# A recorded instruction list with its own list scheduler in place of the framework's, in a fused attention, pooling and memory step

## The chip, the cores and the metric

The kernel is written in Bass/Tile and runs on one core of one Trainium2 chip. Its five instruction streams are PE (TensorE: matmuls and transposes; the profile shows its weight loads apart, as PEld), DVE (VectorE), ACT (ScalarE), POOL (GpSimd) and SP (SyncE, which here only issues DMAs). Each stream is executed in order; between streams an instruction waits on semaphores. What counts is the device time of one execution in microseconds (us).

## The reference, cut to what matters

One layer of a streaming encoder, for a prompt of 1024 frames and a running stream of 64 frames, model width 1024:

```python
h = rmsnorm(x, g_norm) @ w_in                  # q k v gf zf u gp qm gm
F = cumsum(log_sigmoid(zf + b_f))              # forget values, one per head and row
s = q @ k.T * SCALE + F[q] - F[k]; s[k > q] = NEG
fox_o  = softmax(s) @ v                        # 8 heads of 64
pool_o = (window_mean(u, (2, 4, 8, 16)) - u) @ w_pool * pool_scale
mk, mv = split(rmsnorm(mem, g_mem) @ w_mem_kv) # 256 memory tokens
mem_o  = softmax(qm @ mk.T * SCALE) @ mv       # 4 heads of 64
cat = [silu(gf) * fox_o, silu(gp) * pool_o, silu(gm) * mem_o]
y = rmsnorm(x + cat @ w_out, g_final)
```

The 64 frames of the stream (the "sample") attend to 512 cached keys and to themselves. Besides `y`, the keys, values, forget values, memory keys and values and the last rows of `u` are outputs. All is float32.

## The kernel before, in words

**Numbers.** Every large product is made with three matmuls: an operand is split into a high part, rounded to the format fp32r, and the rest (`hi`, `lo`), and hi·hi + hi·lo + lo·hi are added in PSUM (`mm`, L78; `mm3`). ACT makes the high part, DVE or POOL the rest.

**Stages.** (1) Inside `with st`, activations `xT` are loaded and split into `xh`/`xl` in three column chunks, `CH` (256, 512 and 320 columns: prompt and sample together), values are projected with the weights `wv` and stored to the output `v_o`, the forget values are summed (`f_chain1` to `f_chain3`, which leave them in the DRAM tiles `gpd` and `gsd`), and the memory keys and values are made. (2) Twenty projections, each of 128 output rows: four for `q`, four for `k`, four gates `gf`, two `u`, two gates `gp`, two `qm` and two gates `gm` (as a pair, `gmx0`). `load_w` fetches 512 KB of weights into `wr` (two buffers in pool `wp`) and `split_w` makes `whi` and `wlo`; `proj_chunk` adds 24 matmuls into one bank `pp` for each chunk, and an evacuation writes the result to DRAM: `q` to `qd`, `k` to the output `kT_o`, gates to `gated`. `u` stays on the chip. (3) Attention, head by head. `fox_load(h)` reads the head's keys back from `kT_o` and the cache into `kl` and splits them into `ks` (ACT L518, POOL L519), and reads the values into `vraw` and splits them into `vs`. Then one `fox_sample` and four `fox_unit`s of 256 rows: load the bias `nb` from `gpd` (the sample's from `gsd`), add the mask to its last 256 columns (`bm`, POOL), load `qraw` from `qd` and split it into `qh`/`ql`, score matmuls into a bank `s`, add the bias and take the running minimum on DVE (L637), exponential on ACT (L552), divide on DVE (L558), transpose on PE into a bank `pt` (L654), split into `phi` (ACT L563) and `plo` (DVE L564), multiply with `vs` into a bank `o`, and store to the DRAM tile `catd`. Memory heads (`mem_*`) are the same without bias and with 256 keys. (4) `pool_mix(0)` and `(1)`: window sums of `u` on POOL and DVE, five chunks each, and three short matmuls per chunk. (5) `load_wout` loads the output weights in eight pieces and splits them into `wh`/`wl` in the space of `xh`/`xl` (L938); `out_prep` reads `catd` and `gated`, multiplies them and splits the product into `chi`/`clo`; `out_tile` does the output projection, the residual and the last norm of one tile of 128 rows, in the order 8 (the sample), 0, 1, ..., 7.

**Banks and buffers.** PSUM pools `pp` (projections and output), `ps` (scores), `pt` (transposes) and `po` (products) have two banks each. A tile that is asked for takes the oldest buffer of its name, and waits until that one's users are done.

**What sets the order.** The program is written as generators that are stepped against each other. Attention goes through the list `ATT` and after each piece steps a list of fill work, until its cost has caught up with a due value:

```python
FILL = "q0 k0 q1 k1 u0 qm0 q2 k2 q3 k3 qm1 u1 gf0 gf1 gf2 gf3 gp0 gp1 gmx0"
ATT = "f0 f1 f2 f3 m0 m1 m2 m3 f4 f5 f6+f7"
R1, R2, LEAD0, SIDE = 1.25, 2.4, 7.0, 6
```

`R1` and `R2` (for the last group, heads 6 and 7 together) are fill per attention cost; every `SIDE` pieces one chunk of `pool_mix` is stepped. Behind `FILL` stand `load_wout` and the output tiles. That program order is then rescheduled by the framework, `tile.TileContext(nc, schedule_with_timeline_sim=True)`, which chooses from a simulated timeline the order in which each engine gets its instructions.

Of the kernel before, what the change touches and what calls it, by code (L numbers as in the profile page):

```python
# [14 lines left out]
P = 128  # L15
# [10 lines left out]
BIG = 3.0e38  # L26
WARM = 10
CH = [(0, 256), (256, 512), (768, 320)]
LAST = (2, 1, 0)
TQ, TK, TGF, TU, TGP, TQM, TGM = 0, 4, 8, 12, 14, 16, 18  # L30


@with_exitstack
def tile_hymba_step(
# [6 lines left out]
    nc = tc.nc  # L41
    PSUM = bass.MemoryType.PSUM

    cp = ctx.enter_context(tc.tile_pool(name="cp", bufs=1))
    dram = ctx.enter_context(tc.tile_pool(name="dram", bufs=1, space=bass.MemoryType.DRAM))
    pp = ctx.enter_context(tc.tile_pool(name="pp", bufs=2, space=PSUM))
    ps = ctx.enter_context(tc.tile_pool(name="ps", bufs=2, space=PSUM))
    pt = ctx.enter_context(tc.tile_pool(name="pt", bufs=2, space=PSUM))
    po = ctx.enter_context(tc.tile_pool(name="po", bufs=2, space=PSUM))
    big = ctx.enter_context(tc.tile_pool(name="big", bufs=1))  # L50
    wp = ctx.enter_context(tc.tile_pool(name="wp", bufs=2))
    rp = ctx.enter_context(tc.tile_pool(name="rp", bufs=4))
# [3 lines left out]
    fstate = [0, 0.0]  # L56
# [35 lines left out]
    sp = st.enter_context(tc.tile_pool(name="sp", bufs=1))  # L92
# [244 lines left out]

    with st:
        xp = st.enter_context(tc.tile_pool(name="xp", bufs=2))
# [62 lines left out]
        Ts = f_chain1(st.enter_context(tc.tile_pool(name="fp", bufs=1)))  # L402
# [27 lines left out]
        for t in range(2):  # L430
# [12 lines left out]
            nc.sync.dma_start(mv_o[c, :], vr[:, :256])  # L443

    ap_ = ctx.enter_context(tc.tile_pool(name="ap", bufs=2))

    def proj_chunk(w, evac, ci):
        wh, wl = w
        t0, n = CH[ci]
        acc = ppt()  # L450
        trip = []
        for k in range(KT):
            xh, xl = xhi[ci][:, k, :], xlo[ci][:, k, :]
            trip += [(wh[:, k, :], xh), (wh[:, k, :], xl), (wl[:, k, :], xh)]
        mm3(acc[:, :n], trip, 24)
        evac(acc, ci, t0, n)
        return 24 * n / 2400.0

    wq = {}
    tseq = []  # L460

    def get_w(tidx):
        if tidx not in wq:
            wq[tidx] = load_w(wt[tidx], KT, P)
        return wq[tidx]

    def proj(tidx, evac):
        w = get_w(tidx)
        i = tseq.index(tidx)
        for ci in range(3):  # L470
            if ci == 1:
                get_w(tseq[i + 1])
            yield proj_chunk(w, evac, ci)

    def proj2(t1, e1, t2, e2):
        we = [(get_w(t), e) for t, e in ((t1, e1), (t2, e2))]
        for ci in LAST:
            for w, e in we:
                yield proj_chunk(w, e, ci)

    def q_tile(r0):
        def f(acc, ci, t0, n):
            t = row("qr")
            nc.vector.scalar_tensor_tensor(
                t[:, :n], acc[:, :n], SCALE, rb[:, t0 : t0 + n], op0=ALU.mult, op1=ALU.mult
            )
            nc.sync.dma_start(qd[r0 // P][:, t0 : t0 + n], t[:, :n])

        return f

    def k_tile(j):
        def f(acc, ci, t0, n):
            t = row("kr")
            nc.vector.tensor_tensor(t[:, :n], acc[:, :n], rb[:, t0 : t0 + n], op=ALU.mult)
            nc.sync.dma_start(kT_o[j * P : j * P + P, t0 : t0 + n], t[:, :n])

        return f

    def gate_tile(r0):
        def f(acc, ci, t0, n):  # L500
            t = row("gr")
            nc.vector.tensor_tensor(t[:, :n], acc[:, :n], rb[:, t0 : t0 + n], op=ALU.mult)
            th = row("gt")
            nc.scalar.activation(th[:, :n], t[:, :n], AF.Tanh, scale=0.5)
            nc.vector.scalar_tensor_tensor(
                t[:, :n], th[:, :n], 1.0, t[:, :n], op0=ALU.add, op1=ALU.mult
            )
            g, r = divmod(r0, 768)
            nc.sync.dma_start(gated[g][ci][r : r + P, :n], t[:, :n])

        return f
# [91 lines left out]
    def fox_unit(h, c, ks, vs):  # L603
# [16 lines left out]
        for i in (0, 1):  # L620
# [24 lines left out]
            yield 2 * n / 2400.0  # L645
        acc = otile()
        for kp in reversed(range(c + 1)):
# [20 lines left out]
            yield 8 * 0.109  # L668
        finish(acc, par, j * P, 256 * c, 256)

    def fox_sample(h, ks, raw):
# [23 lines left out]
        yield 0.5  # L695
# [11 lines left out]
        yield 1.0  # L707
# [17 lines left out]
    def mem_unit(h, c, km, vm):  # L725
# [12 lines left out]
        yield 0.5  # L738
# [16 lines left out]
        yield 0.9  # L755

    def mem_sample(h, km, raw):
# [22 lines left out]
        yield 0.7  # L780
# [25 lines left out]
    def pool_mix(t):  # L806
        u = UT[t]
        wr = ap_.tile([P, 256], F32, tag="qraw", name=nm("wpr"))
        wh = ap_.tile([P, P], F32R, tag="wph", name=nm("wph"), bufs=1)
        wl = ap_.tile([P, P], F32R, tag="wpl", name=nm("wpl"), bufs=1)  # L810
        nc.sync.dma_start(wr[:, :P], wpool[t])
        nc.scalar.copy(wh, wr[:, :P])
        nc.vector.tensor_tensor(wl, wr[:, :P], wh, op=ALU.subtract)
        al, up = slice(0, P), slice(64, P)
        for a, n, c0 in PM:
# [32 lines left out]
            yield  # L848
            acc = ptt()
# [7 lines left out]
            while b < c0 + n:  # L857
# [4 lines left out]
                b = e  # L862
        done.add(f"w{t}")

    def tl(tidx, mk, *a):
        yield from proj(tidx, mk(*a))

    FILL = "q0 k0 q1 k1 u0 qm0 q2 k2 q3 k3 qm1 u1 gf0 gf1 gf2 gf3 gp0 gp1 gmx0"
    ATT = "f0 f1 f2 f3 m0 m1 m2 m3 f4 f5 f6+f7"
    R1, R2, LEAD0, SIDE = 1.25, 2.4, 7.0, 6  # L870
    SLACK = 12

    cst = [-1]

# [42 lines left out]
    def out_ready(t):  # L917
        return cst[0] >= (0 if t == 8 else t // 2 + 1)
# [26 lines left out]
    def out_tile(t):  # L945
# [8 lines left out]
        if i < 9 and out_ready(order[i]):  # L954
            prep[order[i]] = out_prep(order[i])
# [245 lines left out]
```

## Time and profile before

| quantity | value |
|---|---|
| time, three runs | 671.74, 672.5, 672.58 us; median 672.5 |
| profiled execution | 668.75 us |
| its span, first to last instruction | 667.0 us |
| mean granted TensorE clock | 0.953 of full speed |
| data moved | 93.30 MB, mean 140 GB/s; 110194 packets on the queue that carries nearly all of it |
| loads of `qraw` from `qd` | 48 of 128 KB (q of 128 x 256), and smaller ones for the samples |
| attention units that load `qraw` | 8 heads x 5 and 4 memory heads x 5 |

The profile gives, for one execution, the busy time of each engine, the chain of work that ended last (followed back from the last instruction through what released each step), and the costliest groups of instructions by line. A row of a single instruction reads: start in us, duration in us, engine, line, operation, output<-inputs, sizes, a count where like rows are joined, and in brackets the idle time of the engine ahead of it and what ended that. A row of a stretch reads: start and end, its length, the busy time of each engine with its count of instructions, the mean granted clock, the share of the DMA engines' time, and GB/s. Weight loads (PEld) run beside matmuls of the same engine.

### The profile page before, as it was taken

The page shows a single profiled execution, that of the slowest core. Times are in us where ns is not written, and L with a number is a line of the kernel's source. Part 1 is how long each engine was busy: PE and PEld are TensorE (multiplying, and loading weights), DVE is VectorE, ACT ScalarE, POOL GpSimd, SP SyncE. Part 2 cuts the span into 40 slices and gives each one's busy share as a digit, 9 for nine tenths or more (in the row PEclk, how much of TensorE's full clock was granted, in tenths as well). Part 3 has the DMA queues.
Part 4 walks back from the last instruction along what each step waited for, and adds up shares of the span by engine and source line. Part 5 has one row for each costly group of instructions (what it writes and reads, how often), then busy time and mean ns, then how long its engine had stood idle before and what let it go on. Part 6 is the DMA issues. An engine that isn't in the chain of part 4 may idle for free.

```text
span 667.0 us, 11515 instructions
## 1 busy us (share of the span) xinstructions
PE 589.2 (88%) x3810; PEld 532.8 (80%) x3810; DVE 424.5 (64%) x1124; ACT 307.6 (46%) x713; POOL 214.3 (32%) x285
## 2 busy tenths in 40 slices
PE   8999996959889869998889868889999759999996
PEld 6999895859788769888678757879888648899895
DVE  6957020637778576687688746977877658743434
ACT  5657111525355345355565644745654436522212
POOL 3104513425234242230432413743442244322200
PEclk9999998879899969999899899989999988999999
DMA  8996423554455534623223365356445745665521
GB/s 301 302 316 206 137 88 123 104 136 103 116 111 147 97 110 124 133 78 105 76 56 108 95 128 144 94 131 167 124 122 137 176 134 170 185 195 185 175 95 63
DMA packets 110542, 93.30 MB, mean 140 GB/s; under 512 B 31498, under 2 KB 94930, under 8 KB 110482
## 3 DMA queue, kind: packets, MB, share of 16 engines
q1 hardware_dynamic: 110194, 92.30, 50.4%
q8 instruction: 30, 0.49, 0.3%
q10 hardware_dynamic: 288, 0.27, 0.1%
q14 instruction: 30, 0.25, 0.1%
HBM read 70.68 MB, written 21.86 MB: 139 GB/s over the span
## 4 chain that ended last, share of the span: by engine, by line
DMA 36%; PE 31%; DVE 12%; issue 7%; ACT 6%; POOL 5%; SPq 3%; DVEq 0%; ACTq 0%; POOLq 0%
PE pp L78 23%; DMA nb<-gpd 9%; DMA qraw<-qd 8%; DMA vraw<-out_dram 3%; PE s L78 3%; DMA nat<-in_xn_dram 3%; PE o L78 3%; PE pt L654 2%; DVE P L558 2%; DMA catd<-og 2%; DMA nb<-gsd 2%; DMA wr<-in_wout_dram 2%; ACT P L552 2%; DVE P L637 2%; DVE plo L564 2%
## 5 line engine op out<-in xcount | busy, mean ns | idle before, releaser
L78 PE MATMUL pp<-xh,wlo 128*128 128x256 f32 (+2 forms) x480 | 163.0, 340 | 1.9 <-POOL wlo L158 1.9
L78 PE MATMUL pp<-xh,whi 128*128 128x256 f32 (+2 forms) x480 | 162.8, 339 | 0.1
L78 PE MATMUL pp<-xl,whi 128*128 128x256 f32 (+2 forms) x480 | 162.6, 339 | 0.0
L78 PEld LDWEIGHTS pp<-xh,wlo 128*128 128x128 f32 x480 | 94.7, 197 | 8.8 <-POOL wlo L158 2.4
L78 PEld LDWEIGHTS pp<-xh,whi 128*128 128x128 f32 x480 | 94.7, 197 | 6.8 <-issue 0.3
L78 PEld LDWEIGHTS pp<-xl,whi 128*128 128x128 f32 x480 | 94.6, 197 | 6.1
L552 ACT ACTIVATE P<-P,m 128x128 f32<-128x128 f32 (+8 forms) x72 | 55.9, 776 | 67.3 <-DVE m L637 65.4
L558 DVE TENSOR_SCALAR P<-P,rinv 128x256 f32<-128x256 f32 (+9 forms) x108 | 75.0, 703 | 2.2
L78 PE MATMUL pp<-wh,chi 128*128 128x256 f32 (+1 forms) x208 | 68.4, 331 | 6.6 <-ACT wh L938 5.4
L614 POOL TENSOR_TENSOR bm<-nb,mask 128x256 f32<-128x256 f32 x32 | 25.2, 786 | 151.9 <-DMA nb<-gpd 118.8
L78 PE MATMUL pp<-wl,chi 128*128 128x256 f32 (+1 forms) x208 | 67.7, 328 | 0.5 <-POOL wl L940 0.5
L564 DVE TENSOR_TENSOR plo<-pt,phi 128x512 fp32r<-128x512 f32 (+1 forms) x96 | 60.7, 638 | 11.3 <-ACT phi L563 10.7
L78 PE MATMUL o<-phi,vs 128*128 128x256 f32 x160 | 46.5, 298 | 19.9 <-ACT phi L563 10.3
L78 PE MATMUL pp<-wh,clo 128*128 128x256 f32 (+1 forms) x184 | 59.3, 322 | 0.0
L158 POOL TENSOR_TENSOR wlo<-wr,whi 128x1024 fp32r<-128x1024 f32 x20 | 48.4, 2419 | 31.4 <-ACT whi L157 29.9
L78 PE MATMUL s<-ks,qh 128*128 128x512 f32 (+4 forms) x112 | 42.9, 385 | 15.8 <-DVE m L637 7.9
L563 ACT CAST phi<-pt 128x512 fp32r<-128x512 f32 (+1 forms) x96 | 51.1, 546 | 7.9 <-PE pt L654 6.8
L78 PEld LDWEIGHTS o<-phi,vs 128*128 128x128 f32 x160 | 31.6, 197 | 23.6 <-ACT phi L563 9.2
L78 PEld LDWEIGHTS pp<-wh,chi 128*128 128x128 f32 x208 | 40.7, 196 | 10.6 <-ACT wh L938 5.8
L78 PE MATMUL o<-plo,vs 128*128 128x256 f32 x160 | 43.8, 297 | 3.9 <-DVE plo L564 3.9
L654 PE MATMUL pt<-ident,P 128*128 128x128 f32 x288 | 45.0, 278 | 2.4 <-DVE P L558 2.2
L539 ACT CAST qh<-qraw 128x256 fp32r<-128x256 f32 (+1 forms) x60 | 23.1, 386 | 51.2 <-DMA qraw<-qd 45.6
(254 smaller groups left out, 1305.8 us busy)
## 6 DMA issues: line engine op xcount, KB each, us to landing
wr<-in_wt_dram SPq DMA_DIRECT2D x20, 512.0 KB
qraw<-qd SPq DMA_DIRECT2D x48, 128.0 KB
ct<-catd SPq DMA_DIRECT2D x17, 256.0 KB
nat<-in_xn_dram SPq DMA_DIRECT2D x8, 512.0 KB
nb<-gpd SPq DMA_DIRECT2D x8, 512.0 KB
wr<-in_wout_dram SPq DMA_DIRECT2D x8, 512.0 KB
xt<-in_xn_dram SPq DMA_DIRECT2D x16, 256.0 KB
out_dram<-xt SPq DMA_DIRECT2D x14, 256.0 KB
```

What stands on the lines that cost most here:

```text
L78: nc.tensor.matmul(out, lhsT=lhsT, rhs=rhs, start=start, stop=stop)
L158: (eng or nc.gpsimd).tensor_tensor(lo[:, :n], raw[:, :n], hi[:, :n], op=ALU.subtract)
L539: nc.scalar.copy(qh[:, :n], raw[:, :n])
L552: nc.scalar.activation(Pt[:rows, :n], Pt[:rows, :n] if src is None else src, AF.Exp, bias=m, scale=-1.0 if src is None else 1.0, accum_out ...
L558: nc.vector.tensor_scalar(Pt[:rows, :n], Pt[:rows, :n], ri[:rows], None, op0=ALU.mult)
L563: nc.scalar.copy(hi[:, a:b], src[:, a:b])
L564: nc.vector.tensor_tensor(lo[:, a:b], src[:, a:b], hi[:, a:b], op=ALU.subtract)
L614: nc.gpsimd.tensor_tensor(bm, nb[:, nk - 256 : nk].rearrange("p (a b) -> p a b", a=2), mask.unsqueeze(1).to_broadcast([P, 2, P]), op=ALU.add,)
L637: nc.vector.tensor_tensor_reduce(out=Pt[:, b0:b1], in0=s[:, b0 - a : b1 - a], in1=bm[:, i, :] if src is None else nb[:, b0:b1], scale=-1.0 ...
L654: nc.tensor.transpose(tp[:, jj * 256 + i * P : jj * 256 + i * P + P], pts[i][:, kt * P : kt * P + P], ident,)
```

## The change

Every instruction is no longer issued when the program reaches it. `nc` is now a `Planner`; `nc.vector.x(...)` and the like append an `Op` with its engine, its arguments, a duration, a latency behind it, and its predecessors: earlier operations on overlapping boxes of a tile where one of the two writes, and, for a buffer that is used again, all users of the tile that had it before. `flush` then plans all recorded operations on a model of the five engines and emits them in the order of their planned starts, under `tc.manual_schedule()`, where the framework adds the semaphores and keeps the order. Among the operations of one engine that are ready it takes the one that can start first, then by rank (-1 is called urgent here: matmuls into `ps`, `pt` and `po`, non-tensor operations on `pp`, and anything that writes into the pool `wp`), then by the longest path to the end.

`flush` is called twice: at the end of `with st`, after projections 0 and 1 of `q` and `k` and the weight loads of `u0` and `u1` have been recorded, and at the end for all the rest. The recorded order sets only the rings of buffers (who waits for whom); `FILL` and the pacing constants are gone. For each entry of `ATT` the projections it needs, its loads, its sample and its four units are recorded, then a `pool_mix` whose `u` has been projected, then one projection of `u0 u1 gf0 gf1 gf2 gf3 gp0 gp1 gmx0`; at the end `load_wout` and the output tiles. So `q3` and `k3` are recorded with heads 6 and 7, behind all gates, and `u1` behind head 1.

Three edits are not order: the accumulator of `pool_mix` is a `pp` bank and no longer a `pt` bank; its raw weight has a tile of its own, `wpr` (one buffer), and no longer one of the two of `qraw`; and `out_tile` no longer calls `out_prep` for the tile behind it. All instructions of the changed kernel carry one line number, L243.

```diff
+MARGIN = 0.4
...
+    def add(self, eng, fn, args, kw):
...
+        urgent = into & {"ps", "pt", "po"} if eng == "tensor" else "pp" in homes or "wp" in into
+        op.rank = -1 if urgent else 0
...
+    def cost(self, op, writes, reads):
...
+        op.lat = 0.10
+        if e == "tensor":
...
+                op.dur = max(0.108, 0.008 + 0.000435 * n)
+            op.lat = 0.25
+        elif fn == "dma_start":
...
+            op.dur = 0.45
+            op.bytes = total / (4 * run) / k * (0.009 + 4 * run / 27300)
+            op.lat = 1.9 + op.bytes
+        elif e == "vector":
...
+            op.dur = 0.2 + 0.00054 * n if fast else 0.15 + 0.00104 * n
...
+        elif e == "scalar":
+            op.dur = 0.19 + 0.00084 * n
...
+            op.dur = 0.15 + (0.0004 if fn == "memset" else 0.00218) * n
+            op.port = fn != "memset"
+
+    def flush(self, margin):
...
+                for op in waiting[e]:
+                    t = max(self.free[e], op.ready)
+                    if op.port:
+                        t = max(t, lock["gpsimd" if e == "vector" else "vector"])
+                    late = 0.2 if op.mode is not None and op.mode != self.mode else 0.0
+                    key = (t + late, op.rank, -op.level, op.seq)
...
+            if op.bytes is not None:
+                self.dma = max(self.dma, op.end) + op.bytes
+                op.lat = self.dma - op.end + 1.9
...
+                gap = 0.0 if same else op.lat
+                if s.eng == "tensor" and not same:
+                    gap += margin
+                s.ready = max(s.ready, op.end + gap)
...
+        done.sort(key=lambda o: o.start)
+        with self.tc.manual_schedule():
+            for op in done:
+                getattr(getattr(self.nc, op.eng), op.fn)(*op.args, **op.kw)
...
-            yield
-            acc = ptt()
+            acc = ppt()
             mm(acc[:, :n], wh, hi[:, :n], True, False)
...
+        for j in (0, 1):
+            proj(TQ + j, q_tile(j * P))
+            proj(TK + j, k_tile(j))
+        for t in (TU, TU + 1):
+            get_w(t)
+        f_chain3(gps)
+        nc.flush(MARGIN)
...
+    extra = iter("u0 u1 gf0 gf1 gf2 gf3 gp0 gp1".split())
+    mixed = []
+    for name in ATT.split():
+        group([(x[0], int(x[1])) for x in name.split("+")])
+        while mixed:
+            pool_mix(mixed.pop())
+        project(next(extra, "gmx0"))
+        mixed += [j for j in (0, 1) if f"u{j}" in done and f"p{j}" not in done]
+        done.update(f"p{j}" for j in mixed)
+    load_wout()
+    for t in order:
+        out_tile(t)
+    nc.flush(MARGIN)
```

The order that results differs from before nearly everywhere. Three places, in which a number behind a name only tells tiles of one name apart:

SP's queue at the start of the program, before; `xr` are raw activations, `wr` raw weights (`in_wv` of the values, `in_wt` of the twenty projections):

```order
L349 DMA xr_148<-in_xT_dram 128x2x320
L181 DMA wr_150<-in_wv_dram 128x528
...
L181 DMA wr_173<-in_wv_dram 128x528
...
L401 DMA icnt<-in_icnt_d_dram 128x32
L401 DMA zall<-in_clogf_dram 128x4x8
L167 DMA wr_1064<-in_wt_dram 128x1024
L167 DMA wr_1098<-in_wt_dram 128x1024
```

The same queue, now:

```order
L243 DMA wr_245<-in_wt_dram 128x1024
L243 DMA wr_254<-in_wt_dram 128x1024
L243 DMA wr_132<-in_wv_dram 128x528
L243 DMA xr_131<-in_xT_dram 128x2x320
...
L243 DMA wr_135<-in_wv_dram 128x528
```

The first two projection weights went from rows 25 and 26 of the queue to its first two rows, ahead of the activations.

PE in the first attention stretch, before; `s` are scores of head 0, `pp_1377` and `pp_1422` projections (their inputs are `xh`/`xl` and split weights):

```order
L78 MATMUL s_1328<-ks_1291,qh_1322 128x288
L78 MATMUL s_1328<-ks_1291,ql_1323 128x288
L78 MATMUL s_1333<-ks_1291,qh_1322 128x288
L78 MATMUL s_1333<-ks_1291,ql_1323 128x288
L78 MATMUL pp_1377<-xh_139,wlo_1204 128x320
L78 MATMUL pp_1377<-xh_139,whi_1203 128x320
L78 MATMUL pp_1377<-xl_142,whi_1203 128x320
...
L78 MATMUL pp_1422<-xh_137,whi_1345 128x256
L78 MATMUL pp_1422<-xl_140,whi_1345 128x256
L78 MATMUL pp_1422<-xh_137,wlo_1346 128x256
```

PE in the same stretch now; `pp_1749` is a chunk of `pool_mix` (inputs `ph`, `pl` and its weights `wph`, `wpl`):

```order
L243 MATMUL s_1466<-ks_1452,ql_1462 128x288
L243 MATMUL s_1480<-ks_1452,qh_1477 128x256
L243 MATMUL s_1480<-ks_1452,ql_1478 128x256
L243 MATMUL s_1485<-ks_1452,qh_1477 128x256
L243 MATMUL s_1485<-ks_1452,ql_1478 128x256
L243 MATMUL s_1502<-ks_1452,qh_1499 128x384
L243 MATMUL s_1508<-ks_1452,qh_1499 128x512
L243 MATMUL pp_1749<-ph_1747,wph_1735 128x256
L243 MATMUL pp_1749<-pl_1748,wph_1735 128x256
L243 MATMUL pp_1749<-ph_1747,wpl_1736 128x256
L243 MATMUL s_1502<-ks_1452,ql_1500 128x384
```

Behind the first scores stood long projections; now scores of several units follow each other, and chunks of `pool_mix` stand in the `pp` banks between them.

PE near the last projections, before; `pp_6642` is a gate projection of the pair `gmx0`, `ks_5943` and `ks_5918` are the keys of the last two heads:

```order
L78 MATMUL s_6455<-ks_5943,qh_6400 128x512
L78 MATMUL s_6455<-ks_5943,ql_6401 128x512
L78 MATMUL pp_6642<-xh_139,whi_6579 128x320
L78 MATMUL pp_6642<-xl_142,whi_6579 128x320
L78 MATMUL pp_6642<-xh_139,wlo_6580 128x320
...
L78 MATMUL s_6542<-ks_5918,qh_6537 128x320
L78 MATMUL o_6078<-pc_6076,vraw_5961 64x64 x5
```

PE at the last projection now; `pp_2830` is `k3`, `ks_2677` the keys of head 5, `ks_2834` those of head 6, which are made from `k3`:

```order
L243 MATMUL pp_2830<-xh_121,whi_2826 128x512
L243 MATMUL pp_2830<-xl_124,whi_2826 128x512
L243 MATMUL pp_2830<-xh_121,wlo_2827 128x512
L243 MATMUL pt_2695<-ident,P_2688 128x64 x5
L243 MATMUL pt_2739<-ident,P_2732 128x128
...
L243 MATMUL s_2786<-ks_2677,qh_2783 128x512
L243 MATMUL s_2786<-ks_2677,ql_2784 128x512
...
L243 MATMUL s_2796<-ks_2677,ql_2784 128x512
L243 MATMUL o_2738<-phi_2740,vs_2682 128x256
...
L243 MATMUL s_2853<-ks_2834,qh_2850 128x288
```

Gate projections stood between the scores of the last two heads; now `k3` is the last projection, and some twenty rows of head 5 lie between it and the first score of head 6.

435 lines of the change are left out of this document (265 added, 170 removed).

## The prediction

> **What bounds the kernel now.** I read the page's engine totals first, then the chain that ended last, then busy time by stage, then single rows for paces and prices.
>
> ```profile
> span 667.0 us, 11515 instructions
> ...
> PE 589.2 (88%) x3810; PEld 532.8 (80%) x3810; DVE 424.5 (64%) x1124; ACT 307.6 (46%) x713; POOL 214.3 (32%) x285
> ...
> DMA 36%; PE 31%; DVE 12%; issue 7%; ACT 6%; POOL 5%; SPq 3%; DVEq 0%; ACTq 0%; POOLq 0%
> ```
>
> TensorE looks 88% busy, yet only 31% of the chain is TensorE: it waits for short chains in which transfers are the longest link. The 88% also flatters, because a matmul's record is longer than its slot:
>
> ```profile
> 81.03 0.39 PE L78 MATMUL pp<-xl,whi 128*128 128x512 f32 x1
> 81.25 0.39 PE L78 MATMUL pp<-xh,wlo 128*128 128x512 f32 x1
> ...
> 87.07 0.28 PE L78 MATMUL pp<-xh,whi 128*128 128x256 f32 x1
> 87.19 0.28 PE L78 MATMUL pp<-xl,whi 128*128 128x256 f32 x1
> ```
>
> Starts are 0.23 and 0.12 us apart for 512 and 256 columns, and in proportion between them. I call a row at this spacing paced work (transposes at 0.11). All matmul rows, the same set in both kernels, add to 544 us paced. So 667 - 544 = 123 us are lost to gaps, half clock and changes between matmuls and transposes, and an order can win at most that. By stage:
>
> ```profile
> 25.00:50.00 25.00, 24.46 (x203) 24.04 (x202) 16.28 (x45) 14.80 (x30) 0.00 (x0) 1.00 0.93 305
> ...
> 100.00:125.00 25.00, 18.15 (x101) 16.80 (x101) 4.12 (x10) 7.90 (x14) 13.57 (x12) 0.80 0.44 117
> ...
> 117.30:170.00 52.70, 45.97 (x275) 42.24 (x276) 32.02 (x103) 24.79 (x54) 22.41 (x29) 0.85 0.53 116
> 170.00:250.00 80.00, 68.04 (x422) 60.71 (x422) 55.99 (x157) 36.04 (x86) 28.33 (x44) 0.91 0.49 115
> 250.00:300.00 50.00, 48.40 (x328) 43.80 (x326) 36.19 (x102) 23.56 (x55) 14.19 (x22) 1.00 0.47 112
> 300.00:450.00 150.00, 125.68 (x788) 112.07 (x787) 112.32 (x300) 83.15 (x228) 53.60 (x62) 0.95 0.41 104
> ...
> 425.00:450.00 25.00, 21.07 (x130) 19.09 (x129) 21.34 (x58) 11.99 (x30) 15.51 (x17) 0.93 0.48 120
> 450.00:525.00 75.00, 73.12 (x488) 66.34 (x487) 61.39 (x179) 44.43 (x104) 26.56 (x44) 1.00 0.55 148
> 525.00:563.00 38.00, 25.20 (x138) 22.05 (x137) 22.39 (x46) 16.43 (x30) 15.89 (x12) 0.82 0.56 145
> 563.00:667.00 104.00, 96.84 (x629) 88.00 (x629) 50.16 (x116) 29.57 (x73) 19.19 (x17) 0.99 0.47 149
> ```
>
> Columns: time, then PE, PEld, DVE, ACT, POOL, granted clock, DMA share, GB/s. The first 117 us are projections. From 117.3 to 563 attention runs with projection matmuls as fill, and from 563 the output projection is dense. From 250 to 525 the 1,604 PE rows are 229 us paced, 0.83 of the time; in 450 to 525 they are 71 of 75, 0.95. The best vector window is 21.34 of 25, 0.85. So neither engine is full in 300 to 450: the order is what holds both. The widest loss is 525 to 563.
>
> **The change, part by part.** The instructions are the same; I cut the new order at five places, and count for each stretch its paced TensorE work and its vector rows at their groups' means, such as this one's:
>
> ```profile
> L558 DVE TENSOR_SCALAR P<-P,rinv 128x256 f32<-128x256 f32 (+9 forms) x108 | 75.0, 703 | 2.2
> ```
>
> All vector rows so added give 485 us, and the engine was busy 424.5 (records overlap), so each sum is taken times 0.875. PE / DVE: start to first score 126 / 61; to the first gate projection 50 / 74; to the first matmul of the last q projection (`q3`) 212 / 166; to head 7's first score 27 / 24; to the last score 49 / 60; to the end 80 / 39.
>
> *Start.* Two 512 KB weight loads now stand ahead of the first activations on SP's queue.
>
> ```profile
> 3.85 1.01 ACT L195 ACTIVATE xh<-xr,gn_s 128x320 fp32r<-128x320 f32 x2 [1.16 <-DMA xr<-in_xT_dram]
> ...
> 5.44 0.67 PE L78 MATMUL s<-whi,xh 128*128 128x264 f32 x1
> ...
> 110.12 0.31 PE L78 MATMUL pp<-xl,whi 128*128 128x320 f32 x1
> 117.28 0.61 PE L78 MATMUL s<-ks,qh 128*128 128x288 f32 x1 [6.85 <-POOL ks L519]
> ```
>
> At 305 GB/s, 1.05 MB is 3.4 us, and nothing covers it, since TensorE's work up to 70 us is dense behind its first matmul at 5.44. The first score comes after 126 us of paced work instead of 103: +23. That extra work (all of projection `u0`) stands where TensorE idled 6.85 us for the keys, and I take that gap as covered: 117.3 + 3.4 + 23 - 6.9 = 137. With the gap kept it is 144; with the loads hidden, 134.
>
> *First attention stretch, 50 / 74.* Heads 0 and 1 and both pooling paths now run with only `u1` as fill, and `u1` must wait in the ring of two `pp` banks behind four pooling chunks. Vector becomes the bound: at 0.85, 74 becomes 87 us. At the share of 117 to 250 now, (32.02 + 55.99)/132.7 = 0.66, it is 112; at 0.92 it is 80. I take 0.85: with two pooling chains and two heads there are more independent vector rows at hand than in the best window.
>
> *Middle, 212 / 166.* Fill always stands behind each score and transpose; the stretch of before that is like it is 450 to 525. At 0.93, a little under its 0.95, it is 228 us; at 0.95, 223; at the 0.83 of 250 to 525, 255.
>
> *`q3`/`k3` and head 6, 27 / 24.* Before, gate projections stood beside the last two heads; now `k3` is the last projection, and after it TensorE has 12 us of paced attention rows before the first score that needs `k3`. That score waits for keys that go to DRAM and back:
>
> ```profile
> 105.90 5.42 DMA out_dram<-kr
> 112.49 2.65 DMA kl<-in_ckT_dram
> 115.17 0.77 ACT ks L518 x2
> 115.97 1.26 POOL ks L519
> ...
> 163.40 7.17 DMA kl<-out_dram
> ...
> 180.93 9.91 DMA nb<-gpd
> ```
>
> 5.42 + 2.65 + 0.77 + 1.26 = 10 us at best, 15 with 7.17 for the load, against 12 of cover; and SP issues some 20 transfers between. I put 28 at pace (27/0.95) and 7 of stall: 35, bounds 28 and 45.
>
> *Last scores, 49 / 60.* Both heads' units with output tiles as fill. Vector is the bound: 60/0.91 = 66; at 0.82, the share of 450 to 525, 73; at 1.0, 60.
>
> *End, 80 / 39.* Dense as now: from 575 on before had 81 us paced left and took 92, so 91 (90 to 92).
>
> ```profile
> 546.77 0.80 PE L78 MATMUL pp<-wh,chi 128*128 128x512 f32 x1 [5.42 <-ACT wh L938]
> ```
>
> This wait for the split output weights goes: their matmuls now come 17 us of paced work after the last projection, which is cover for eight 1.05 us copies. Without it, 5.4 more.
>
> Sum: 137 + 87 + 228 + 35 + 66 + 91 = 644 us of span. What lies around the span is 668.75 - 667.0 = 1.75, and the median of the runs, 672.5, stands 3.75 above the profiled run: 650. Nothing is priced for the pooling accumulators that move from `pt` to `pp` (ten short ones) beyond the wait of `u1`, nor for the smaller `wpr` tile: both lie beside vector-bound work.
>
> The planner books 1.9 us plus the bytes for a transfer; the rows above show 2.65 to 9.91. The Trainium skill, "DMA: Bandwidth & Descriptors", section "Anatomy of one DMA", gives about 2.0 us fixed plus bytes at 436 GB/s, fitted on another issue path. By it the fourth stretch would have no stall and the whole would be 643; the trace's small strided loads take three to four times that, and the measurement decides.
>
> **The rivals.** *Late transfers (slower).* Score and key rows stand in an in-order queue where the planner expected their data, 4 to 6 us too early by the rows above. There are 60 units that load `qraw` (8 heads by 5, 4 memory heads by 5). The forecast leaves some 22 us to the time before, so a mean stall of 0.4 us per unit decides; at 0.75 it is 45 us: 695. For it: in 100 to 125 and 525 to 563, where fill ran out, TensorE was busy only 18.15 of 25 and 25.20 of 38 us. Against it: the planner issues loads as early as the double buffers allow, and fill is deep in the middle stretch.
>
> *Half clock in the sparse stretch.* In 100 to 125 the clock averaged 0.80 behind a gap of 6.85 us. If all of the first attention stretch ran at half clock, its 50 us would take 100, 13 over the 87: 663. By the Trainium skill, "TensorE: Matmul & The Clock Gate", "Part 1: The HAM clock gate", one idle window of about 3.4 us halves the clock and a busy one restores it. The 0.80 window agrees; by that rule it comes if the sparse rows leave whole windows idle.
>
> *Full overlap.* If both engines reach the best shares everywhere (80, 223, 28, 60, 90 and 134) the span is 615: 621. For it: 450 to 525 holds weight loads for 66.34 of 75 us, nearly the density of 563 on, with vector at 0.82 beside it.
>
> *A draw.* The middle stretch at 0.85 (249) gives back 21 of the 22 won: 672.
>
> **How the numbers follow.** Forecast 650, chance 0.45, its own range 635 to 665; half clock 0.07; full overlap 0.15; draw 0.05; late transfers 0.28. Faster is the first three, 0.67. The range is 615 to 700. A measurement of this kernel tells about 0.2% from no change.
>
> **What would show it.** First matmul near 8.9 us and first score near 137; vector over 0.8 and weight loads under 0.6 in the 87 us behind it; weight loads over 0.85 in the middle; a gap of some 5 us behind the last projection; the last 80 us as dense as now. Wrong: weight-load share under 0.8 in the middle with waits for `qraw`, `nb`, `kl` ahead of score matmuls, or a first stretch over 105 us.

## The result, and the profile after

The changed kernel takes 755.6 us (median; 753.7 to 759.8) against 672.25 us: the ratio is 1.125, with a 95% interval of 1.120 to 1.130. The forecast was 650, within 615 to 700. It was wrong in its sign. The profiled execution took 753.68 us with a span of 751.9.

From the page of the changed kernel, the span, the busy times and the chain that ended last, by engine and by line:

```profile
span 751.9 us, 11447 instructions
...
PE 622.0 (83%) x3810; PEld 548.8 (73%) x3810; DVE 409.4 (54%) x1124; ACT 315.2 (42%) x717; POOL 210.7 (28%) x285
...
PE 42%; DMA 34%; DVE 10%; ACT 5%; issue 4%; SPq 3%; POOL 2%; ACTq 0%; DVEq 0%; POOLq 0%
PE pp L243 31%; DMA qraw<-qd 20%; PE s L243 5%; DMA nb<-gpd 4%; SPq L243 3%; PE pt L243 3%; PE o L243 3%; DVE P L243 2%; DMA nat<-in_xn_dram 2%; DMA wr<-in_wv_dram 2%; DMA nb<-gsd 2%; DMA catd<-cat 1%; ACT P L243 1%; ACT qh L243 1%; DVE ql L243 1%
```

TensorE and VectorE have as many instructions as before (3810 and 1124), and VectorE is even busy for 15 us less. The line to look at is `qraw<-qd`: it is 20% of the chain, 148 us in 23 pieces. Before it was 8%:

```profile
PE pp L78 23%; DMA nb<-gpd 9%; DMA qraw<-qd 8%; DMA vraw<-out_dram 3%; PE s L78 3%; DMA nat<-in_xn_dram 3%; PE o L78 3%; PE pt L654 2%; DVE P L558 2%; DMA catd<-og 2%; DMA nb<-gsd 2%; DMA wr<-in_wout_dram 2%; ACT P L552 2%; DVE P L637 2%; DVE plo L564 2%
```

The busy times by stage, cut at the forecast's places (columns: PE, PEld, DVE, ACT, POOL, granted clock, DMA share, GB/s), and the rows that make the cuts:

```profile
145.00:248.00 103.00, 63.63 (x330) 51.98 (x329) 65.26 (x198) 49.37 (x116) 48.76 (x73) 0.74 0.41 99
248.00:514.00 266.00, 233.34 (x1435) 207.87 (x1435) 150.50 (x435) 117.37 (x299) 62.35 (x75) 0.94 0.36 97
514.00:562.00 48.00, 41.27 (x260) 35.43 (x259) 30.39 (x92) 21.97 (x51) 16.65 (x24) 0.97 0.50 142
562.00:659.00 97.00, 68.57 (x378) 58.33 (x377) 58.50 (x170) 50.16 (x104) 36.21 (x45) 0.77 0.53 141
659.00:752.00 93.00, 82.13 (x522) 73.03 (x520) 43.54 (x97) 25.00 (x61) 12.21 (x10) 0.97 0.37 121
```

```profile
8.19 0.39 PE L243 MATMUL s<-whi,xh 128*128 128x264 f32 x1 [2.44 <-ACT xh L243]
...
144.90 0.30 PE L243 MATMUL s<-ks,qh 128*128 128x288 f32 x1
...
247.67 0.41 PE L243 MATMUL pp<-xh,whi 128*128 128x256 f32 x1
...
562.51 0.44 PE L243 MATMUL s<-ks,qh 128*128 128x288 f32 x1
...
658.57 0.48 PE L243 MATMUL s<-ks,ql 128*128 128x512 f32 x1
```

They are the first value matmul, the first score, the first gate projection (found by its place in the program's order, as is `q3`), head 7's first score and the last score. The cut at 514 lies some 3 us behind `q3`'s first row, at 511.07; cut there, the middle is 263 us and the stretch behind it 51, and no reading below changes by that.

| stretch | forecast (bounds) | measured |
|---|---|---|
| start to first score | 137 (134 to 144) | 144.9 |
| first attention stretch | 87 (80 to 112) | 102.8 |
| middle | 228 (223 to 255) | 266 |
| `q3` to head 7's first score | 35 (28 to 45) | 48.5 |
| last scores | 66 (60 to 73) | 96.1 |
| end | 91 (90 to 92) | 93.3 |
| sum | 644 | 751.9 |

All six lie above the value taken, and all but the first attention stretch above the upper bound, the start and the end by about 1 us. None of these stretches between 145 and 659 is as dense as 450 to 525 was before (weight loads 0.88 there, 0.78 now in the best, the middle). In the hollow stretches neither PE nor DVE is full, and the granted clock is down to 0.74 and 0.77.

How a late transfer spreads is seen in the changed kernel's timeline around 330 us:

```profile
325.89 1.24 SPq L243 DMA_DIRECT2D qraw<-qd  x2
...
330.21 0.54 PE L243 MATMUL pp<-xh,wlo 128*128 128x320 f32 x2
331.97 0.30 ACT L243 CAST qh<-qraw 128x128 fp32r<-128x128 f32 x1 [2.86 <-DMA qraw<-qd]
332.17 1.15 ACT L243 ACTIVATE P<-P,m 128x1024 f32<-128x1024 f32 x1
332.30 0.29 DVE L243 TENSOR_TENSOR ql<-qraw,qh 128x128 fp32r<-128x128 f32 x1 [2.04 <-ACT qh L243]
332.32 0.39 PE L243 MATMUL s<-km,qh 128*128 128x256 f32 x1 [1.57 <-ACT qh L243]
332.51 0.68 DVE L243 TENSOR_SCALAR P<-P,rinv 128x896 f32<-128x896 f32 x1
```

The two halves of a sample's `qraw` are issued from 325.89 on, and the copy that waits for them starts at 331.97, 6 us later; ACT stands at it for 2.86 us. Behind it in ACT's queue is an exponential of another unit that does not use that `qraw`; on DVE `ql` waits 2.04 us for ACT, with a division of another unit behind it; PE waits 1.57 us, with transposes of another unit's `P` and projections behind. One transfer that the plan had too early stops three in-order engines.

### The profile page after: what moved, and what is told of

It is laid out like the page before. It is cut to its first block, busy times and chain, and to the rows that moved or that the text cites. A ratio compares the mean times of both kernels' runs of the same rounds, so it can differ in the third digit from the quotient of the medians.

```text
span 751.9 us, 11447 instructions
## 1 busy us (share of the span) xinstructions
PE 622.0 (83%) x3810; PEld 548.8 (73%) x3810; DVE 409.4 (54%) x1124; ACT 315.2 (42%) x717; POOL 210.7 (28%) x285
## 4 chain that ended last, share of the span: by engine, by line
PE 42%; DMA 34%; DVE 10%; ACT 5%; issue 4%; SPq 3%; POOL 2%; ACTq 0%; DVEq 0%; POOLq 0%
PE pp L243 31%; DMA qraw<-qd 20%; PE s L243 5%; DMA nb<-gpd 4%; SPq L243 3%; PE pt L243 3%; PE o L243 3%; DVE P L243 2%; DMA nat<-in_xn_dram 2%; DMA wr<-in_wv_dram 2%; DMA nb<-gsd 2%; DMA catd<-cat 1%; ACT P L243 1%; ACT qh L243 1%; DVE ql L243 1%
## 5 line engine op out<-in xcount | busy, mean ns | idle before, releaser
L243 PE MATMUL pp<-xh,whi 128*128 128x512 f32 (+2 forms) x480 | 152.4, 344 | 6.8 <-DVE gr L243 2.5
L243 PE MATMUL pp<-xl,whi 128*128 128x512 f32 (+2 forms) x480 | 150.2, 338 | 0.0
L243 PE MATMUL pp<-xh,wlo 128*128 128x512 f32 (+2 forms) x480 | 148.3, 338 | 0.1
L243 PEld LDWEIGHTS pp<-xh,whi 128*128 128x128 f32 x480 | 90.7, 196 | 15.4 <-DVE gr L243 3.2
L243 PEld LDWEIGHTS pp<-xh,wlo 128*128 128x128 f32 x480 | 90.0, 196 | 6.4 <-POOL wlo L243 0.3
L243 PEld LDWEIGHTS pp<-xl,whi 128*128 128x128 f32 x480 | 90.8, 196 | 5.1
L243 PE MATMUL pt<-ident,P 128*128 128x128 f32 (+1 forms) x400 | 72.9, 294 | 23.3 <-DVE P L243 16.4
L243 POOL TENSOR_TENSOR wlo<-wr,whi 128x1024 fp32r<-128x1024 f32 (+1 forms) x24 | 55.8, 2328 | 118.6 <-ACT whi L243 98.1
L243 DVE TENSOR_TENSOR plo<-pt,phi 128x512 fp32r<-128x512 f32 (+1 forms) x96 | 60.4, 639 | 39.0 <-ACT phi L243 37.8
L243 PEld LDWEIGHTS pt<-ident,P 128*128 128x128 f32 (+1 forms) x400 | 51.1, 152 | 34.3 <-DVE P L243 17.5
L243 ACT CAST phi<-pt 128x512 fp32r<-128x512 f32 (+1 forms) x96 | 51.6, 547 | 51.5 <-PE pt L243 41.5
L243 PE MATMUL s<-ks,qh 128*128 128x512 f32 (+4 forms) x112 | 45.7, 417 | 30.9 <-DVE m L243 20.5
L243 PE MATMUL pp<-wh,chi 128*128 128x256 f32 (+1 forms) x208 | 65.3, 337 | 7.0 <-ACT pp L243 6.7
L243 ACT CAST qh<-qraw 128x256 fp32r<-128x256 f32 (+1 forms) x60 | 22.9, 383 | 111.7 <-DMA qraw<-qd 99.3
L243 PE MATMUL o<-phi,vs 128*128 128x256 f32 x160 | 49.0, 320 | 23.0 <-ACT phi L243 16.5
L243 ACT ACTIVATE P<-P,m 128x256 f32<-128x256 f32 (+8 forms) x72 | 55.6, 773 | 26.0 <-DVE m L243 25.8
L243 PE MATMUL pp<-wl,chi 128*128 128x256 f32 (+1 forms) x208 | 64.0, 331 | 0.0
L243 POOL TENSOR_TENSOR bm<-nb,mask 128x256 f32<-128x256 f32 x32 | 24.5, 764 | 111.8 <-DMA nb<-gpd 102.8
L243 PE MATMUL pp<-wh,clo 128*128 128x256 f32 (+1 forms) x184 | 55.6, 328 | 0.0
L243 DVE TENSOR_TENSOR ql<-qraw,qh 128x256 fp32r<-128x256 f32 (+1 forms) x60 | 25.8, 440 | 53.3 <-ACT qh L243 53.0
L243 DVE TENSOR_SCALAR P<-P,rinv 128x256 f32<-128x256 f32 (+9 forms) x108 | 53.5, 514 | 1.3
L243 PEld LDWEIGHTS s<-ks,qh 128*128 128x128 f32 x112 | 24.1, 218 | 40.1 <-issue 15.7
```

The lines of the kernel that those rows point to most:

```text
L243: getattr(getattr(self.nc, op.eng), op.fn)(*op.args, **op.kw)
```

## The experiments

All times are medians beside runs of the kernel before on the same chip (668.4 to 669.8 us; 670.8 for the last). The theories: A, the planner's 1.9 us per transfer is too short, so waiting rows stand ahead of ready ones; B, the recorded order leaves too little fill beside some heads; C, half clock feeds on itself.

**The planner's latency.** The edit, with 6.0 and with 9.0:

```diff
+DLAT = 6.0
-            op.lat = 1.9 + op.bytes
+            op.lat = DLAT + op.bytes
-                op.lat = self.dma - op.end + 1.9
+                op.lat = self.dma - op.end + DLAT
```

> The planner's fixed latency of a transfer goes from 1.9 to 6.0 us (both places), near what the chain of the changed kernel shows for qraw (24 pieces, mean 6.5 us, bytes included). Nothing else changes. Theory A (late transfers: score rows are planned before their data can be there, so TensorE stands behind them): the planner now puts other rows into these times; ACT's wait for qraw falls from 99 us to about the 46 of before, and the time from 755 to 660-690. Theory B (record order: too little fill beside heads 0 and 1 and beside heads 6 and 7, whatever the latency says): the first attention stretch stays near 103 us and the last scores near 96, and the time is 735-755. Theory C (half clock feeds on itself): in between, 700-735, with the granted clock still near 0.90.

> The same with 9.0 us, above the mean and near the longest pieces of the chain (qraw 9.14, nb 9.60 us). Theory A: as good as with 6.0 or a little better, 655-690, since the slow transfers are covered too; if the latency alone were the cause but covered at 6.0, within 1% of that run. Theory B: 735-760, no trend with the latency. Theory C: 700-740.

692.9 us with 6.0 (ratio to before 1.035, 1.029 to 1.040), 696.3 with 9.0 (1.037, 1.030 to 1.045). So 63 of the 83 us come from this constant, and more than 6.0 brings nothing: this is A's direction, but both times lie above A's ranges (690 at most), so it is not all of the loss. B, which had the first attention stretch stay near 103 us, does not hold alone: from the first score (158.21) to the first gate projection (236.58) it is now 78. The chain has 23 pieces of `qraw`, mean 6.4 us; the 24 and 6.5 of the expectation are slightly off. What ACT waited for `qraw` (us in total, times, longest), in the kernel before, in the changed kernel, and with 6.0:

```profile
ACT qh L539 <- DMA qraw<-qd: 45.6, 21, 5.5
```

```profile
ACT qh L243 <- DMA qraw<-qd: 99.3, 40, 5.9
```

```profile
ACT qh L244 <- DMA qraw<-qd: 26.2, 19, 4.2
```

And by stage with 6.0 (columns as above):

```profile
150.00:275.00 125.00, 92.56 (x522) 77.88 (x523) 92.36 (x273) 66.39 (x158) 59.12 (x90) 0.84 0.45 112
275.00:500.00 225.00, 219.30 (x1443) 198.46 (x1443) 157.94 (x429) 118.03 (x298) 63.92 (x76) 0.99 0.45 115
500.00:600.00 100.00, 73.50 (x411) 60.52 (x410) 72.97 (x194) 54.70 (x117) 40.51 (x50) 0.80 0.62 154
```

Between 275 and 500 PE is now dense at a clock of 0.99. Two holes are left, behind the first scores and beside the last two heads.

**Planner and record apart.** One run has the unchanged planner on the program of before (generators, `FILL`, pacing; its first plan ends ahead of `q0`); the other has the changed program with `nc` the plain object, ordered by the framework.

```diff
-    nc = Planner(tc.nc, tc)
+    nc = tc.nc
...
-    nc.flush(MARGIN)
```

> The planner, unchanged (1.9 us), on the program of before: its recorded order, rings, early prefetches and pooling accumulators are those of the kernel before (FILL, ATT, pacing), and only the choice of the issue order is the planner's. The first of the two plans ends ahead of the first projection here. Theory A: the planner's short latency is the cause wherever the record comes from, so it is slow too, 715-760. Theory B: the record order is the cause, so the old record brings it back to 640-685.

> The changed kernel's program (record order, pooling accumulators in pp, wpr) issued at once and ordered by the framework's scheduler, with no planner. Theory A: the planner is the cause, so this is near the time of before, 665-700. Theory B: the record order is the cause, so this is slow, 720-800. If the framework's scheduler needs fill close by in program order to find it, it is slow under A as well, and only a fast result decides.

703.9 us (1.049, 1.045 to 1.054) and 734.1 us (1.095, 1.090 to 1.100). The first lies between the ranges of the two theories, the second in that of B: neither theory alone allows both. By its expectation a slow second run does not decide by itself, but under the planner the two records differ too: 755.6 against 703.9. The planner costs 34 us on the old program, and the record costs 64 under the framework, together 83 and not 98. In the first ACT waits for `qraw` as in the changed kernel:

```profile
ACT qh L243 <- DMA qraw<-qd: 102.3, 33, 9.7
```

**Both put right.**

> The planner with 6.0 us per transfer on the program of before (the run with 1.9 us on it was 704 us against 670 of before). Two separate causes (the planner's short latency, which cost 34 there, and the record order, which cost 64 under the framework's scheduler): the latency's part goes and the time is 655-680. If planner and framework differ by something else as well (the start, where the planner is 8 to 10 us of paced TensorE work behind at 75 us in all its runs), it stays at 680-690. If the latency matters only on the new record: 695-710.

656.8 us, ratio 0.983 (0.978 to 0.988): 1.7% below before. The latency's part goes, 47 us, and the hole is not there. The same stretch as above in this run:

```profile
150.00:275.00 125.00, 123.70 (x829) 112.72 (x830) 93.50 (x284) 63.87 (x146) 51.70 (x75) 1.00 0.54 141
```

PE has 829 rows there against 522. So each of the two causes is there without the other, though their shares do not add up. What in the record does that was the next question.

**First guesses at the record.** All three with 6.0 us: the pooling accumulator back in `pt`; a record with projections moved into both holes (each entry is recorded behind one entry of `ATT`; P0 and P1 are `pool_mix`); and writes into `wp` no longer urgent.

```diff
-            acc = ppt()
+            acc = ptt()
```

```diff
+        "u0 q2 k2", "P0 q3 u1", "k3 P1", "gf0", "gf1", "", "gf2", "", "gf3", "gp0", "gp1 gmx0"
```

```diff
-        urgent = ... else "pp" in homes or "wp" in into
+        urgent = ... else "pp" in homes
```

> The changed kernel with 6.0 us, and the pooling accumulator back in a pt bank, so that projections need not wait in the ring of pp behind pooling chunks. With 6.0 us alone it was 693, with a hole between 150 and 275 us in which paced TensorE work was 0.30 to 0.68 of the time. Theory ring (the pp banks hold the fill back): the next projections fill the hole, 665-680. Theory record (there is nothing to fill with: the second u needs the buffer of the first, and the gates stand behind it in the ring anyway): 685-695.

706.5 us, 14 slower: outside both ranges. PE now waits up to 7.38 us at a pooling matmul (at 249.56), and between 231 and 273 us, while the five chunks pass through the `pt` banks and behind them, it runs no transpose. My reading is that the ring holds back whatever shares it, in `pp` or in `pt`; this run alone does not prove it.

> The changed kernel with 6.0 us and another record order: behind head 0 u0, q2, k2; head 1 pooling of u0, q3, u1; head 2 k3, pooling of u1; then one gate behind each of heads 3, mem 0, mem 2, 4 and 5, and the last gates (gp1, gmx0) behind heads 6 and 7; the weights loaded in the first plan are those of u0 and q2. So both stretches that were hollow have projections to fill them. Theory record (the two holes at 150-275 and 500-600 us are what is left of the loss): TensorE's paced work there rises to about 0.9, about 30 and 25 us come back, 635-660, faster than before. If the holes are the waits of the heads themselves and not lack of fill: 680-695.

694.6 us, no gain, the range of the other theory; yet the hole was filled, as the first row shows:

```profile
150.00:275.00 125.00, 111.27 (x703) 96.96 (x701) 95.48 (x298) 70.73 (x164) 61.32 (x88) 0.97 0.54 131
307.00:346.00 39.00, 36.76 (x221) 32.79 (x221) 11.14 (x15) 5.32 (x10) 4.79 (x2) 1.00 0.25 75
500.00:575.00 75.00, 55.82 (x316) 44.71 (x317) 59.67 (x183) 46.41 (x108) 28.47 (x45) 0.86 0.56 146
```

The second row points to the reason: for 39 us PE runs almost only projections (DVE 11.14 of 39), and `qm0` is recorded directly ahead of the memory heads. The fill is used up without attention beside it, and attention then runs without fill in the third.

> The changed kernel with 6.0 us, and operations that write into the pool wp no longer urgent: the two 512 KB weight loads leave the head of SP's queue. By the prediction's term the start gains 3.4 us: first matmul of values at 5.5 instead of 9.3 us. If later weight loads then come late (they lose their rank everywhere), the gain is lost again in the middle: 690-705. Otherwise 687-692.

681.0 us (1.017, 1.014 to 1.021), 12 less than with the rank, where 1 to 6 were expected. The first value matmul comes 2.75 us earlier (6.53 instead of 9.28) and the first score 8.4 us earlier (149.80 instead of 158.21), so a good part of it is seen by then; that the early loads alone make it was not shown.

**The end of the first plan.** In the changed kernel the first plan's rows on SP stand ahead of all loads of head 0, down to `k1`'s last store:

```profile
133.45 0.82 SPq L243 DMA_DIRECT2D out_dram<-kr  x2
134.37 0.39 SPq L243 DMA_DIRECT2D gsd<-gts  x1
...
137.83 0.49 SPq L243 DMA_DIRECT2D kl<-in_ckT_dram  x1
138.37 0.60 SPq L243 DMA_DIRECT2D qraw<-qd  x1
```

My theory was that this delays attention, a long chain, by its 25 us. The edit ends the first plan ahead of the four projections:

```diff
+        nc.flush(MARGIN)
...
-        nc.flush(MARGIN)
```

> The changed kernel (1.9 us) with one edit: the first plan ends before the projections of q0, k0, q1 and k1 are recorded, so that they and head 0's loads are planned together. In the changed kernel all of SP's rows of the first plan, down to the store of k1's last chunk at 133.45 us and the forget values behind it, stand ahead of head 0's loads (from 137 us), and the first score comes at 144.9 us instead of 117.28. Theory boundary (attention is a long chain whose start sets its end: 444 us from first to last score before, 435 with 6.0 us): first score near 120 us, and the time falls by the 25 us or so: 725-735. Theory record (the hole behind the first scores is lack of fill): first score earlier, but the same work is then missing later, 745-755.

> The same edit with 6.0 us per transfer (693 without the edit). Theory boundary: the two costs are separate and both go, 660-670, a little faster than before. Theory record: 682-693.

> As the run before, and writes into the pool wp no longer urgent. Without the edit of the boundary that gave 12 us (693 to 681), of which the start showed some 3 at 75 us; the early weight loads are gone here already. If the other 9 came from SP, ACT and POOL serving weights ahead of attention's rows: 650-660. If all of it was the start: equal to the run before within 1%.

> The planner with 6.0 us on the program of before (657 us), and writes into wp no longer urgent. If the weights' rank delays attention's rows here as well: 645-652. If only the start of the changed kernel suffered from it: 655-660.

753.9 with 1.9 us, 691.5 with 6.0, 691.9 with the rank gone too: nothing. The theory fell. The first score did come earlier with 6.0, at 134.79 instead of 158.21, and then attention paused (the scores behind these stand at 138.80, the next at 158.57):

```profile
134.79 0.29 PE L244 MATMUL s<-ks,qh 128*128 128x288 f32 x1
...
158.57 0.28 PE L244 MATMUL s<-ks,qh 128*128 128x256 f32 x1
```

On the program of before, with the rank gone, the planner reaches 644.6 us, ratio 0.962 (0.957 to 0.967), the best of all runs. No early weight loads exist there, so the rank costs 12 us there for another reason, which I did not find.

**The order of the projections, and the pooling in pieces.** The changed kernel with projections recorded as in `FILL`, each head's own ones well ahead of it:

```diff
+    plan = (
+        "u0 qm0", "q2 k2 P0", "q3 k3", "qm1 u1", "P1 gf0", "gf1", "gf2", "gf3", "gp0", "gp1", "gmx0"
+    )
```

It is read as above; the first plan loads the weights of `u0` and `qm0`.

> The changed kernel with 6.0 us and the projections recorded in the order of before's FILL: behind head 0 u0 and qm0, head 1 q2, k2 and the pooling of u0, head 2 q3 and k3, head 3 qm1 and u1, then the pooling of u1 and one gate per group, gmx0 last; the first plan loads the weights of u0 and qm0. Theory just-in-time (in the changed record each head's own projections stand directly ahead of it, so attention pauses while they run, 39 us at the first memory head in the run that filled the hole, and the fill is used up): the pause and the hole both go, 650-668. Theory pieces (the old record wins by how finely attention and fill are interleaved in it, not by the order of the projections): 680-695.

> The same record with the planner's own 1.9 us: the changed kernel with the order of its projections alone undone. If the order of the projections is what the record costs: near the 704 of the planner on the program of before, 695-715. If the short latency dominates: 735-755.

> The record of FILL with 6.0 us, and writes into wp no longer urgent. On the old record that gave 12 us (657 to 645), on the changed record 12 us with its early weight loads and nothing without them. If it is the early loads: 640-658 here, where they exist; if not, equal to the run with FILL within 1%.

679.7 with 6.0, 721.8 with 1.9 (1.078, 1.075 to 1.081), 670.2 without the rank. The order of the projections, with the places of the poolings that go with it, is worth 34 us at 1.9 and 13 at 6.0, so the shares do not add up. Both times are above what the theory gave (668 and 715 at most), 679.7 at the lower edge of the other: the order of the projections is one part only, and against the program of before 18 to 26 us stayed in each of the three. The 670.2 lies outside both of its ranges.

> The run before (FILL order, 6.0 us, writes into wp not urgent, 670 us) with the first plan ending ahead of q0, k0, q1 and k1. On the changed record that edit gave nothing, with 1.9 us and with 6.0. If that was because the fill was then missing later, it pays here, where fill is there: 645-658, near the 645 of the same planner on the program of before. If an earlier first score is worth nothing: 665-675.

> The same with the pooling accumulator back in a pt bank. On the changed record with 6.0 us that cost 14 us (693 to 707), with a wait of 7.4 us of a pooling matmul ahead of transposes. If the choice of bank matters by itself: 10 to 15 us over the run before. If it only mattered where fill was missing: within 4 us of it.

681.6 and 683.5 us, the first outside both ranges: the end of the first plan is not the rest (earlier is 11 slower here), and the bank alone makes 2 us, less than the spread of the runs. Last, the chunks in pieces: `pool_mix` is a generator again, stepped behind each sample and unit of a head.

```diff
-            acc = ppt()
+            yield
+            acc = ptt()
...
+                side()
```

> FILL order, 6.0 us, writes into wp not urgent (670 us), and the five chunks of each pooling no longer recorded in a row: one chunk behind each sample or unit of the next head, its accumulator in a pt bank, as before did. In a row they sit between projections in the two pp banks, or between two heads' transposes in the two pt banks. If that is what is left of the record's cost (paced TensorE work is 0.63 to 0.71 of the time at 200-275 and 325-350 us, just where the poolings run): 645-658. If not: 665-680, and the rest stays open.

646.8 us, ratio to before 0.963 (0.958 to 0.969), 23 less than with five chunks in a row (670.2) and 2 from the planner on the program of before. In a row, then spread:

```profile
200.00:275.00 75.00, 65.95 (x415) 56.93 (x414) 58.03 (x186) 42.74 (x102) 27.82 (x46) 0.95 0.53 125
325.00:350.00 25.00, 22.20 (x128) 19.76 (x129) 21.77 (x65) 18.37 (x59) 5.65 (x10) 0.80 0.33 90
```

```profile
200.00:275.00 75.00, 74.04 (x493) 66.56 (x492) 53.53 (x165) 39.41 (x89) 30.14 (x43) 1.00 0.52 144
325.00:350.00 25.00, 24.63 (x173) 22.18 (x172) 20.96 (x52) 17.74 (x54) 8.70 (x8) 1.00 0.35 107
```

PE does 493 rows instead of 415 in the first window. A ring of two banks is served in the recorded order, and five chunks in a row, each waiting for its window sums, close it to everything recorded behind them. The rows of `pp` show it: in a row, no projection matmul runs from 207.0 to 234.0 us, nor from 316.4 to 339.9, while pooling chunks pass and for some microseconds behind; spread, projections run between the chunks. The edit also moved the accumulator to `pt`; the two runs ahead of it make the bank alone worth 2 us, if that holds with this end of the first plan too.

What the changed kernel pays, in medians: the program of before 703.9, 656.8 and 644.6 (1.9 us; 6.0; 6.0 and no rank for `wp`); the order of `FILL` with the changed kernel's pooling 721.8, 679.7 and 670.2; the changed record 755.6, 692.9 and 681.0.

## Why the prediction was wrong, step by step

Two steps failed. The sum left out late transfers, which cost 63 us here, and it priced the recorded order at little more than the wait of `u1` and 7 us of stall behind `k3`, where with 6.0 us it costs 36 us against the program of before (692.9 and 656.8). By stretches:

- **"Late transfers (slower)"** was the rival with a chance of 0.28 at 695 us. The mechanism is shown: 63, 42 and 47 us on three records. Its price was too low: with 60 units, 63 us is 1.05 us per unit and not 0.75. And it was set against the forecast as an alternative, while the record's loss comes on top. The bound of 700 held only one of the two.
- **The middle, 228 us (223 to 255), measured 266.** The step that failed is "at 0.93, a little under its 0.95": between 247.67 and 511.07 the changed kernel has 208 us of paced work, 0.79 of the time. The share came from a stretch that the framework had ordered, and the argument against late transfers, that loads are issued as early as the buffers allow, speaks of the loads and not of the rows that wait for them. With 6.0 us PE is busy for 219.30 of 225 us, and the weight loads for 0.88, so the density that I took is there once the plan knows the transfers.
- **The first stretch, 87 us ("vector becomes the bound"), measured 102.8.** It was never vector-bound: DVE was busy for 65.26 of 103 us. I saw that `u1` "must wait in the ring of two `pp` banks behind four pooling chunks" and took it as a matter of little fill; but while those chunks pass, no projection runs at all: none from 145.9 to 187.5 us and none from 215.4 to 247.7. "Nothing is priced for the pooling accumulators" beyond that wait was the mis-sized term: it is not the change of bank, but five chunks recorded in a row are 23 us, with the order of `FILL` and 6.0 us.
- **`q3`/`k3`, 35 us (28 to 45), measured 48.5.** The 27 us of paced work were counted too low: `q3` and `k3` alone are 144 rows, 24 us at the prediction's pace, and from 511.07 to 562.51 TensorE has 41 us. (The first stretch has 43 and not 50, the middle 208 and not 212; the sum of the three was about right.) The 7 us of stall for the keys did not come where it was priced: head 6's first score, at 554.38, has no idle time ahead of it. What was right is that projections directly ahead of their head cost something; I priced that at one place, and it stands at the memory heads and head 4 as well (39 us at the first memory head in one run).
- **Last scores, 66 us, measured 96.1.** Again not vector: DVE 58.50 of 97. The projections had ended at 548.51 us, and beside two heads only output tiles were left, which need their results.
- **The start, 137, measured 144.9**, just over the bound in which the gap for the keys is kept. The first matmul at 8.19 was forecast near 8.9. With 6.0 us, the first value matmul comes 2.75 us earlier when the two early loads leave the head of the queue, so 3.4 us for their bytes was a fair price there. That the rank costs 12 us in all is more than this, and it costs 12 us on the program of before too, which has no such loads; why stays open.
- **The end, 91, measured 93.3.** Right to 1.3 us above its bound.
- **Half clock.** 0.74 and 0.77 in the hollow stretches, down to 0.50 from 154.51 to 162.32 us, where TensorE had two rows; 0.968 over the whole of the run with spread pooling. In the run with the `pt` bank, behind the wait of 7.38 us, rows of 320 columns start 0.27 us apart from 252.1 to 257.2 us and 0.16 apart right behind that, so a slower pace does follow such gaps. Since no run changes the clock alone, its own share stays open.

By the Trainium skill, "DMA: Bandwidth & Descriptors", section "Anatomy of one DMA", a transfer takes about 2.0 us fixed plus bytes, a fit on another issue path than this kernel's. The changed kernel's chain has 23 pieces of `qraw<-qd` from 4.01 to 9.14 us, mean 6.4. A plan with nearly the skill's figure is the changed kernel; one with 6.0 is 63 us faster. The measurement decides.

## What to carry to other kernels

In these runs a static order on in-order queues was only as good as its estimates: a transfer booked 4 us short stopped the engine that waited, and through it ready work behind on two more. So take transfer times for a planner from the chain of waits of a trace under load, and err upwards (9.0 instead of 6.0 cost nothing that can be told here). And a scheduler that may choose any order is still bound by the rings: here, recording what shares a ring of two buffers in pieces, each near the time at which it can run, saved 23 us, and recording what a stage needs well ahead of it saved 13 to 34 us.

## What the runs showed of the hardware that I had not expected

The `qraw` loads on the changed kernel's chain (128 KB, and smaller ones of the samples) take 4 to 9 us, and not because the DMA engines are full: in the 23 pieces these are busy for 0.11 to 0.71 of the time, and the piece at 332.62 took 6.53 us at 0.11, the one at 464.42 only 4.01 us at 0.51. What makes them late was not found. And VectorE's division of `P` fell from 703 to 514 ns (mean of 108 rows, the same shapes) in the changed kernel, whose planner keeps some VectorE and GpSimd rows apart:

```profile
L243 DVE TENSOR_SCALAR P<-P,rinv 128x256 f32<-128x256 f32 (+9 forms) x108 | 53.5, 514 | 1.3
```

It is 512 ns with the planner's 1.9 us on the program of before, 584 with 6.0 us, and 583 under the framework on the changed record, so how much of it the planner's rule makes was not shown.
